# Turning the normalised gate input with DRAM loads and VectorE block transposes instead of TensorE

## The chip, the cores and the metric

The kernel runs on one core of a Trainium2 chip. The metric is the device time of one execution in microseconds (us); the median of several executions is given. A profile of one execution shows what each engine did: PE is TensorE's matmuls, PEld its weight loads, DVE VectorE, ACT ScalarE, POOL GpSimd, SP the engine that issues most transfers.

## The reference

One decoder layer on 1024 prompt tokens and 8 sample tokens, model width 1024. The part that matters here is its end:

```python
    m = (sigmoid(g_a) * (y_a @ w_pa) + sigmoid(g_b) * (y_b @ w_pb))
    h = h + rmsnorm(m @ w_out, post_g)
    e = p @ w_ple
    gate = sigmoid(rmsnorm(h, ple_in_g) @ w_pg)
    h = h + rmsnorm(gate * e, ple_out_g)
    # rmsnorm(x, g) = x * rsqrt(mean(x * x) + EPS) * g, over the 1024 features
```

Before it stand the input projection to seven branches, chunked gating, pooling and the merge. The outputs are `h` and some states.

## The kernel before, in words

All tensors are float32. A product is computed as three TensorE products of parts: each operand is split into a high part (`h` at the end of its name) by ACT and the rest (`l`) by DVE, and `split` issues both. Large products use Strassen's scheme with seven steps, P1 to P7, for a pair of 128-row tiles; each step is twelve matmuls in the last two stages, and the combinations of operands that it needs are named T1 to T4, B11, B21, B22 (of the moving operand) and S1 to S4, A11 and so on (of the stationary one).

The last two stages are the output projection (`outsteps`, the weights `wo`, whose parts are woB11, woT3 and so on) and the gate (`gatesteps`, the weights `wg`). Both go over four pairs of token tiles. The moving operand is the weight matrix, whose seven parts lie in buffers, high and low, for the whole stage (28 buffers). The stationary operand is the activation with its features on partitions: `Turned` reads it from `big`, a tile of 128 partitions x 8 feature blocks x tokens, where block `k` and partition `p` hold one feature. For the output projection that is the merged `m` (tiles `ms`, `mw`); for the gate it is the normalised `h` (tiles `hs`, `hw`). While the last pair of the output projection runs, the wo parts are given up one by one and the wg parts are loaded and split into the free buffers (`turn_over`); some of the sums of wg's blocks were stored in DRAM far earlier by `column_steps` (`wglow`, `wghigh`).

When a pair of the output projection is done, `out_finish` scales each token tile by its norm and the gain row `post`, adds the residual with an accumulating transfer on POOL's queue and stores `h` to DRAM. One step later `gate_norm` takes the mean square of `h` (ACT) and multiplies `h` by the reciprocal root (DVE), giving `hn`, with tokens on partitions. Five steps after that `gate_input` turns `hn` to features on partitions: eight TensorE transposes of 128x128 into PSUM (tiles `pht`), and eight ACT copies into `big` that multiply by the gain `ple_in_g`, held as a column per feature block in `gvec`. The sample tokens (tile `S`, 8 rows) go through `sample_stationary`.

The instructions are not issued in program order. All calls are recorded by `Planner`, which then works out an order for each engine from estimated durations, due times and dependences, and issues that fixed order (`play`); therefore nearly all instructions carry the one line L290, and tile names tell them apart. Loads and intermediate tiles take buffers from one pool of 46 (`slot`). A step has a time `at` which the planner works from; an instruction is not started more than 14 us before it is due, and a transfer on SP's queue keeps its place in SP's order and waits there for what it needs. PSUM has three regions for step results (`acc`, `acct`) and two single banks (`bank`: pht, psst, sps and others).

Of the kernel before, what the change touches and what calls it, by code (L numbers as in the profile page):

```python
# [8 lines left out]
F32 = mybir.dt.float32  # L9
F32R = mybir.dt.float32r  # L10
BF16 = mybir.dt.bfloat16
AF = mybir.ActivationFunctionType
ALU = mybir.AluOpType

P = 128
D = 1024
NB = D // P
SEQ = 1024
NS = 8
T = SEQ + NS  # L20
HALF = 512
QUART = 256
# [274 lines left out]
def hybrid_step(  # L297
# [7 lines left out]
    nc = tc.nc  # L305
    cpool = ctx.enter_context(tc.tile_pool(name="consts", bufs=1))
    spool = ctx.enter_context(tc.tile_pool(name="slots", bufs=SLOTS))
    small = ctx.enter_context(tc.tile_pool(name="small", bufs=20))
    dram = ctx.enter_context(tc.tile_pool(name="spill", bufs=1, space=bass.MemoryType.DRAM))
# [11 lines left out]
    def slot(name, shape=(P, T), dt=F32):  # L321
        n_name[0] += 1
        return plan.tile(spool.tile(list(shape), dt, tag="slot", name=f"{name}_{n_name[0]}", bufs=SLOTS,
                                    padded_shape=None), "slot")
# [5 lines left out]
    def bank(name):  # L330
        n_name[0] += 1
        return plan.tile(bankp.tile([P, 512], F32, tag="bank", name=f"{name}_{n_name[0]}"), "bank")
# [8 lines left out]
    def split(src, hi, lo):  # L341

        nc.scalar.activation(out=hi, in_=src, func=AF.Copy)
        nc.vector.tensor_tensor(out=lo, in0=src, in1=f32(hi), op=ALU.subtract)

    def dma(out, in_, by=None):
        (by or nc.sync).dma_start(out=out, in_=in_)
# [7 lines left out]
    def mul(out, a, b):  # L355
        nc.vector.tensor_tensor(out=out, in0=a, in1=b, op=ALU.mult)
# [9 lines left out]
    nc = plan  # L366
# [37 lines left out]
    class Operand:  # L404
# [37 lines left out]
        def at(self, what, k):  # L442
            return [part[:, k % 2, :] for part in self.parts[what, k // 2]]

    class Stored(Operand):
# [4 lines left out]

        def __init__(self, name, b, low, high, wide=WIDE, free=None):
            super().__init__(name, wide)
            self.src, self.raw, self.free = {"b": b, "low": low, "high": high}, {}, free or {}

        def load(self, what):
            key, i, j = self.ROWS[what]
            first = self.wide if key == "low" else HALF
            c = slice(first, first + self.wide) if j else slice(0, first)
            for kk in range(2):
                r = (4 * i + 2 * kk) * P  # L460
                w = c.stop - c.start
                if what in self.free:
                    raw = self.free[what][:, kk * 2 * w : (kk + 1) * 2 * w].rearrange("p (k t) -> p k t", k=2)
                else:
                    raw = slot(f"{self.name}{what}", (P, 2, w))
                self.raw[what, kk] = raw
                dma(raw, self.src[key][r : r + 2 * P, c].rearrange("(k p) t -> p k t", p=P))

        def cut(self, what):
            for kk in range(2):  # L470
# [202 lines left out]
    class User:  # L673

        func = AF.Copy
# [104 lines left out]
        nc.vector.tensor_tensor(out=low[:NS, :], in0=ps[:NS, :], in1=low[:NS, :], op=ALU.add)  # L780
        return low

    def sample_stationary(src, nk, gain=None):

        st = slot("sst", (P, nk, P), F32R)
        nc.gpsimd.memset(f32(st), 0.0)
        ps = bank("psst").rearrange("p (k t) -> p k t", t=16)
        for k in range(nk):
            nc.tensor.transpose(ps[:, k, :NS], src[:NS, k * P : (k + 1) * P], ident[:NS, :NS])
        got = ps[:, :nk, :NS]  # L790
        if gain is not None:
            mul(smix_s, got, gain.unsqueeze(2).to_broadcast([P, NB, NS]))
            got = smix_s
        split(got, st[:, :, :NS], st[:, :, 32 : 32 + NS])
        return st


# [48 lines left out]
    S = NB  # L846
# [138 lines left out]
    for key, w in (("ya", WIDE), ("yb", WIDE), ("wo", HALF), ("wg", HALF)):  # L985
        kept[key + "low"] = dram.tile([HALF, 2 * w], F32, tag=key + "low", name=key + "low")
        kept[key + "high"] = dram.tile([HALF, HALF + w], F32, tag=key + "high", name=key + "high")
    kept["h"] = dram.tile([T, D], F32, tag="h", name="h")
    kept["e"] = dram.tile([T, D], F32, tag="e", name="e")

    def spill(key, b, src, by=None):
# [19 lines left out]
    def stored(key, src, width, free=None):  # L1011
        return Stored(key, src, kept[key + "low"], kept[key + "high"], width, free)
# [297 lines left out]
    def column_sums(key, src, b):  # L1310

        lo, hi = raw = [slot(f"{key}raw", (P, D)) for _ in range(2)]
        for i, t in enumerate(raw):
            dma(t, src[(4 * i + b) * P : (4 * i + b + 1) * P, :])
        return lambda: store_sums(key, b, lo, hi, HALF)

    def column_steps(key, src, steps):
# [2 lines left out]
            at(l, lambda b=b, held=held: held.append(column_sums(key, src, b)))  # L1320
            at(c, lambda held=held: held[0]())

    for n, (key, src) in enumerate((("wo", w_out), ("wg", w_pg))):
        column_steps(key, src, [(uflow[8 + 5 * (4 * n + i)], uflow[11 + 5 * (4 * n + i)]) for i in range(4)])

    def sample_product(st, op):
# [48 lines left out]
    def gate_norm(t):  # L1375

        r = rows(t)
        h = h_of.pop(t)
        hn = hn_of[t] = slot("hn", (P, D))
        rs = rstd([square_sum(h[:r], r, scratch=hn)], r)  # L1380
        nc.vector.tensor_scalar_mul(hn[:r], h[:r], rs[:r])

    def gate_input(t):

        hn = hn_of.pop(t)
        if t == S:
            samples["h"] = sample_stationary(hn, NB, gvec[:, 2 * NB :])
            return
        for k4 in range(0, NB, 4):
            ps = bank("pht")  # L1390
            for k in range(4):
                nc.tensor.transpose(ps[:, k * P : (k + 1) * P], hn[:, (k4 + k) * P : (k4 + k + 1) * P], ident)
            for k in range(4):
                nc.scalar.activation(out=big[:, k4 + k, t * P : (t + 1) * P], in_=ps[:, k * P : (k + 1) * P],
                                     func=AF.Copy, scale=col(2, k4 + k))

    def merged_sample():
        st = samples["m"] = slot("mst", (P, NB, P), F32R)
# [76 lines left out]
    LAST = ("P1", "P6", "P7", "P4", "P5", "P3", "P2")  # L1475

    FIRST = ("P1", "P7", "P6", "P2", "P4", "P5", "P3")
    woop, wgop = stored("wo", w_out, HALF), stored("wg", w_pg, HALF)
    outsteps = [strassen(Turned(i, "m"), woop, Out(i), Tokens, None if i else FIRST) for i in range(NPAIR)]
    gatesteps = [strassen(Turned(i, "h"), wgop, Embed(i), Tokens, LAST if i == NPAIR - 1 else None)  # L1480
                 for i in range(NPAIR)]
# [10 lines left out]
    def gain_row(key, src):  # L1492
        gains[key] = row_broadcast(src, key)

    at(pbsteps[3][4], lambda: gain_row("post", post_g[0]))
    at(outsteps[3][4], lambda: gain_row("out", ple_out_g[0]))
    at(outsteps[0][1], merged_sample)
    at(outsteps[1][2], out_sample)
# [69 lines left out]
        dma(rows[:, t : t + 2, n * HALF : (n + 1) * HALF], e)  # L1568

    def embed_sample():  # L1570
        st = sample_stationary(praw[2], 2)
        for n in range(2):
            full = sample_matmul([(st[:, k, :], *we.at(n, k)) for k in range(2)])
            dma(kept["e"][SEQ:T, n * HALF : (n + 1) * HALF], full[:NS])


    def begin():

        psl = slot("psamp", (P, PLE))
        p_load(0)  # L1580
        we.fetch(0, nc.scalar)
        for t in range(4):
            x_load(t)
        for i, v in enumerate((pre_g, pool_scale, ple_in_g)):
            dma(vecs[i * NB : (i + 1) * NB, :], v[0].rearrange("(k p) -> k p", p=P), nc.scalar)
        we.fetch(1)
        steps[0].loads()
        dma(xe[:NS], x_sample)
        for t in range(4, NB):
            x_load(t)  # L1590
        p_load(1)
        dma(psl[:NS], p_sample)
        praw.append(psl)
        steps[4].loads()
        fetched[0] = 5
        early_loads()

        plan.fixed = False
        ps = bank("warm")
        for t in range(10):  # L1600
            nc.tensor.transpose(ps[:, t % 4 * P : (t % 4 + 1) * P], ident, ident)
        p_turn(0)
        we_cut(0)
        for t in range(4):
            norm_root(t)
            norm_scale(t)
        embed(0, 0)
        embed_out(0, 0)
        embed(1, 0)
        embed_out(1, 0)  # L1610
        vps = bank("vecs")
        nc.tensor.transpose(vps[:, : 3 * NB], vecs[: 3 * NB, :], ident[: 3 * NB, : 3 * NB])
        nc.vector.tensor_copy(gvec, vps[:, : 3 * NB])
        we_cut(1)
        embed(0, 1)
        embed_out(0, 1)
        x_half(0, (0, 1))
        xop.cut("B11")
        steps[0].prepare()
        embed(1, 1)  # L1620
        embed_out(1, 1)
        x_half(0, (2, 3))
        xop.cut("B21")
        steps[0].run()
        steps[0].evacuate()
        steps[1].prepare()
        norm_root(S)
        norm_scale(S)
        for t in range(4, NB):
            norm_root(t)  # L1630
            norm_scale(t)
        x_extra()
        steps[1].run()
        steps[1].evacuate()
        p_turn(1)
        embed(2, 0)
        embed_out(2, 0)
        x_half(1, (0, 1))
        xop.cut("B12")
        embed(2, 1)  # L1640
        embed_out(2, 1)
        x_half(1, (2, 3))
        xop.cut("B22")
        embed(3, 0)
        embed_out(3, 0)
        prepared[0] = 4
        small_tables()
        steps[2].run()
        steps[2].evacuate()
# [5 lines left out]
        we.drop(0)  # L1655
        we.drop(1)

    gvec = cpool.tile([P, 3 * NB], F32, tag="gvec", name="gvec")
    begin()
    for s in range(3):  # L1660
        for f in steps[s].after:
# [34 lines left out]
```

## Time and profile before

| | |
|---|---|
| time, median of 3 runs | 1005.81 us (1005.71 to 1006.13) |
| profiled execution, its own time: the span from first to last instruction | 1004.0 us; the median of the runs holds 1.8 us more |
| PE busy | 988.3 us in 6186 matmuls |
| DVE busy | 798.0 us in 1239 instructions |
| ACT busy | 489.0 us in 889 instructions |
| POOL busy | 81.0 us in 162 instructions |
| DRAM read, written | 112.49 MB, 47.58 MB |

Busy time is the time in which at least one instruction of the engine is under way; matmuls overlap each other, so their own durations add up to more. In rows of groups the columns are line, engine, operation, output <- inputs, shapes, count | busy us, mean ns of one | idle time before them and what ended it. In rows of a timeline they are start, us, engine, line, operation. In rows of the chain that ended last they are start, us, engine and tile. The output projection runs from about 825 to 907 us, the gate from 900 to the end.

### The profile page before, as it was taken

How to read it: one execution, taken by the hardware profiler on the slowest of the kernel's cores; microseconds unless marked ns; L12 is line 12 of the kernel's file. 1: busy time of each engine (PE TensorE's matmuls, PEld its weight loads, DVE VectorE, ACT ScalarE, POOL GpSimd, SP SyncE). 2: the span in 40 equal slices, each digit the busy share in tenths (PEclk: the TensorE clock that was granted, in tenths of full speed). 3: DMA queues.
4: the chain of work that ended last, by engine and by line, in shares of the span. 5: the costliest groups of instructions: out<-in, count | busy, mean ns of one | idle time of the engine just before them, and what ended most of it. 6: DMA issues, size and time to landing. Idle time of an engine off the chain costs nothing. (4 is left out here: it accounts for less than half of the span.)

```text
span 1004.0 us, 16119 instructions
## 1 busy us (share of the span) xinstructions
PE 988.3 (98%) x6186; PEld 887.4 (88%) x6186; DVE 798.0 (79%) x1239; ACT 489.0 (49%) x889; POOL 81.0 (8%) x162
## 2 busy tenths in 40 slices
PE   8999999999999999999999999999999999998996
PEld 6899999999999999999999999999999988887885
DVE  5697448876779898887776987697799898779796
ACT  7765355555434334232432333562353365678563
POOL 1230001000000000000010100000000002312121
PEclk9999999999999999999999999999999999999998
DMA  9331213222365675441304076973754543397437
GB/s 352 130 107 43 85 43 128 85 85 85 131 225 190 238 269 197 169 169 53 126 13 157 28 251 214 315 281 122 247 218 150 182 152 84 87 306 259 128 75 221
DMA packets 85601, 160.65 MB, mean 160 GB/s; under 512 B 7422, under 2 KB 46382, under 8 KB 85517
## 3 DMA queue, kind: packets, MB, share of 16 engines
q1 hardware_dynamic: 83157, 151.72, 43.1%
q0 software_dynamic: 2048, 7.37, 4.3%
q8 instruction: 48, 0.79, 0.3%
q10 hardware_dynamic: 320, 0.54, 0.2%
q14 instruction: 28, 0.23, 0.1%
HBM read 112.49 MB, written 47.58 MB: 159 GB/s over the span
## 5 line engine op out<-in xcount | busy, mean ns | idle before, releaser
L290 DVE TENSOR_TENSOR u<-acc,u 128x520 f32<-128x520 f32 (+1 forms) x90 | 62.4, 695 | 38.6 <-PE acc L290 34.4
L290 POOL TENSOR_TENSOR rstd<-ms,mhalf 128x1 f32<-128x1 f32 (+1 forms) x45 | 40.7, 907 | 218.4 <-DVE ms L290 196.0
L290 POOL MEMSET u<- 128x8 f32 x35 | 3.7, 105 | 548.9 <-PE acc L290 270.2
L290 ACT ACTIVATE u<-acc 128x512 f32<-128x512 f32 x39 | 23.2, 595 | 35.2 <-PE acc L290 35.0
L290 ACT ACTIVATE paw<-pas 128x512 fp32r<-128x512 f32 x16 | 10.1, 630 | 30.5 <-DVE pas L290 25.2
L290 DVE TENSOR_TENSOR big<-big 128x1024 f32<-128x1024 f32 (+4 forms) x20 | 24.5, 1262 | 0.0
L290 ACT ACTIVATE pbw<-pbs 128x512 fp32r<-128x512 f32 x16 | 10.0, 629 | 28.8 <-DVE pbs L290 25.5
L290 DVE TENSOR_TENSOR xb<-acc,u 128x520 f32<-128x520 f32 (+1 forms) x12 | 8.3, 693 | 19.1 <-PE acc L290 19.1
L290 ACT ACTIVATE zbw<-zbs 128x512 fp32r<-128x512 f32 x16 | 9.9, 628 | 27.4 <-DVE zbs L290 24.1
L290 ACT ACTIVATE big<-vt 128x256 f32<-128x256 f32 x32 | 11.9, 381 | 19.7 <-PE vt L290 19.7
L290 ACT ACTIVATE big<-pht,gvec 128x128 f32<-128x128 f32 x64 | 18.0, 398 | 7.1 <-PE pht L290 7.1
L290 PE MATMUL accm<-qh,wpoolw 128*128 128x260 f32 (+1 forms) x96 | 20.9, 320 | 0.0
L290 ACT ACTIVATE big<-mix 128x256 f32<-128x256 f32 x32 | 12.1, 383 | 17.6 <-PE mix L290 17.2
L290 DVE TENSOR_TENSOR acc<-acc,u 128x512 f32<-128x512 f32 (+1 forms) x16 | 11.2, 697 | 8.8 <-PE acc L290 8.8
L290 ACT ACT_TABLE_LOAD x13 | 16.7, 1283 | 2.6 <-PE acc L290 1.6
L290 DVE TENSOR_TENSOR v<-acc,u 128x520 f32<-128x520 f32 (+1 forms) x9 | 6.2, 693 | 14.4 <-PE acc L290 14.4
L290 PEld LDWEIGHTS accm<-qh,wpoolw 128*128 128x128 f32 x96 | 15.7, 188 | 1.9
L290 ACT ACTIVATE gbw<-gbs 128x512 fp32r<-128x512 f32 x16 | 10.0, 625 | 14.9 <-DVE gbs L290 14.1
L290 ACT ACTIVATE xbw<-xbs 128x512 fp32r<-128x512 f32 x16 | 9.8, 625 | 15.2 <-DVE xbs L290 12.8
L290 DVE SCALAR_TENSOR_TENSOR zb<-accm,gvec,zb 128x512 f32<-128x512 f32 (+1 forms) x16 | 12.0, 751 | 6.5 <-PE accm L290 6.4
L290 DVE TENSOR_TENSOR big<-mix,big 128x256 f32<-128x256 f32 x32 | 13.2, 421 | 4.4 <-ACT big L290 3.6
L290 ACT ACTIVATE uw<-us 128x512 fp32r<-128x512 f32 x16 | 9.8, 628 | 13.5 <-DVE us L290 7.6
(689 smaller groups left out, 3622.2 us busy)
## 6 DMA issues: line engine op xcount, KB each, us to landing
ga<-ga SPq DMA_DIRECT2D x16, 516.0 KB
gb<-gb SPq DMA_DIRECT2D x16, 516.0 KB
ya<-za SPq DMA_DIRECT2D x8, 516.0 KB
yb<-zb SPq DMA_DIRECT2D x8, 516.0 KB
x<-in_x_prompt_dram SPq DMA_DIRECT2D x8, 512.0 KB
vraw<-in_w_in_dram SPq DMA_DIRECT2D x8, 512.0 KB
e<-e SPq DMA_DIRECT2D x8, 512.0 KB
garaw<-in_w_in_dram SPq DMA_DIRECT2D x8, 512.0 KB
```

What stands on the lines that cost most here:

```text
L290: getattr(getattr(self.nc, e), method)(*args, **kwargs)
```

## The change: what it does

`hn` of a prompt tile is multiplied by the root and by the gain in one DVE instruction, with the gain as a row on all partitions (`gains["in"]`, loaded once), and stored to DRAM (`kept["hn"]`). `gate_input` loads it back with four transfers; transfer `j` takes 256 features of the 128 tokens and puts token block `b` (32 tokens each) and token `i` of it at partition `32 j + i`, column block `b`. One DVE instruction then transposes all blocks of 32x32 in place of the 64 TensorE transposes of the eight tiles, writing straight to `big`. Since partition `p` then holds the features `8 p + k`, and no longer `k * 128 + p`, the gate's weights are read with their rows in the same order: `w_gate` is `w_pg` seen as `(p k) m -> p k m`. The sample tile's features are taken in steps of eight, and its gain multiplication in `sample_stationary` goes. The column form of `ple_in_g` goes from `vecs` and `gvec`.

```diff
@@ class Stored
         def __init__(self, name, b, low, high, wide=WIDE, free=None):
             super().__init__(name, wide)
-            self.src, self.raw, self.free = {"b": b, "low": low, "high": high}, {}, free or {}
+            chunks = lambda src: src.rearrange("(k p) t -> p k t", p=P)
+            self.src = {"b": b if len(b.shape) == 3 else chunks(b), "low": chunks(low), "high": chunks(high)}
+            self.raw, self.free = {}, free or {}
...
-                r = (4 * i + 2 * kk) * P
+                r = 4 * i + 2 * kk
...
-                dma(raw, self.src[key][r : r + 2 * P, c].rearrange("(k p) t -> p k t", p=P))
+                dma(raw, self.src[key][:, r : r + 2, c])
@@ sample_stationary
-    def sample_stationary(src, nk, gain=None):
+    def sample_stationary(src, nk):
...
-            nc.tensor.transpose(ps[:, k, :NS], src[:NS, k * P : (k + 1) * P], ident[:NS, :NS])
-        got = ps[:, :nk, :NS]
-        if gain is not None:
-            mul(smix_s, got, gain.unsqueeze(2).to_broadcast([P, NB, NS]))
-            got = smix_s
-        split(got, st[:, :, :NS], st[:, :, 32 : 32 + NS])
+            nc.tensor.transpose(ps[:, k, :NS], src[:NS, k], ident[:NS, :NS])
+        split(ps[:, :nk, :NS], st[:, :, :NS], st[:, :, 32 : 32 + NS])
...
+    kept["hn"] = dram.tile([SEQ, D], F32, tag="hn", name="hn")
@@ column_sums
-            dma(t, src[(4 * i + b) * P : (4 * i + b + 1) * P, :])
+            dma(t, src[:, 4 * i + b])
...
-    for n, (key, src) in enumerate((("wo", w_out), ("wg", w_pg))):
+    w_gate = w_pg.rearrange("(p k) m -> p k m", k=NB)
+    for n, (key, src) in enumerate((("wo", w_out.rearrange("(k p) m -> p k m", p=P)), ("wg", w_gate))):
@@ gate_norm
-        nc.vector.tensor_scalar_mul(hn[:r], h[:r], rs[:r])
+        nc.vector.scalar_tensor_tensor(out=hn[:r], in0=h[:r], scalar=rs[:r], in1=gains["in"][:r],
+                                       op0=ALU.mult, op1=ALU.mult)
+        if t != S:
+            dma(kept["hn"][t * P : (t + 1) * P, :], hn)
@@ gate_input
         if t == S:
-            samples["h"] = sample_stationary(hn, NB, gvec[:, 2 * NB :])
+            samples["h"] = sample_stationary(hn.rearrange("p (f k) -> p k f", k=NB), NB)
             return
-        for k4 in range(0, NB, 4):
-            ps = bank("pht")
-            for k in range(4):
-                nc.tensor.transpose(ps[:, k * P : (k + 1) * P], hn[:, (k4 + k) * P : (k4 + k + 1) * P], ident)
-            for k in range(4):
-                nc.scalar.activation(out=big[:, k4 + k, t * P : (t + 1) * P], in_=ps[:, k * P : (k + 1) * P],
-                                     func=AF.Copy, scale=col(2, k4 + k))
+        blocks = slot("hq", (P, 4, QUART))
+        src = kept["hn"][t * P : (t + 1) * P, :].rearrange("(b i) f -> i b f", i=32)
+        for j in range(4):
+            dma(blocks[32 * j : 32 * j + 32], src[:, :, j * QUART : (j + 1) * QUART])
+        nc.vector.transpose(out=big[:, :, t * P : (t + 1) * P].rearrange("p k (b i) -> p k b i", i=32),
+                            in_=blocks.rearrange("p b (r k) -> p k b r", k=NB))
...
-    woop, wgop = stored("wo", w_out, HALF), stored("wg", w_pg, HALF)
+    woop, wgop = stored("wo", w_out, HALF), stored("wg", w_gate, HALF)
...
+    at(outsteps[0][1], lambda: gain_row("in", ple_in_g[0]))
@@ begin
-        for i, v in enumerate((pre_g, pool_scale, ple_in_g)):
+        for i, v in enumerate((pre_g, pool_scale)):
...
-        nc.tensor.transpose(vps[:, : 3 * NB], vecs[: 3 * NB, :], ident[: 3 * NB, : 3 * NB])
-        nc.vector.tensor_copy(gvec, vps[:, : 3 * NB])
+        nc.tensor.transpose(vps[:, : 2 * NB], vecs[: 2 * NB, :], ident[: 2 * NB, : 2 * NB])
+        nc.vector.tensor_copy(gvec, vps[:, : 2 * NB])
...
-    gvec = cpool.tile([P, 3 * NB], F32, tag="gvec", name="gvec")
+    gvec = cpool.tile([P, 2 * NB], F32, tag="gvec", name="gvec")
```

More of the change, by code (lines that the diff above doesn't have):

```diff
@@ L1570, in embed_sample @@
     def embed_sample():
-        st = sample_stationary(praw[2], 2)
+        st = sample_stationary(praw[2].rearrange("p (k c) -> p k c", k=2), 2)
         for n in range(2):
```

## The prediction

> **What bounds the kernel now.** I read the page's busy times first.
>
> ```profile
> span 1004.0 us, 16119 instructions
> PE 988.3 (98%) x6186; PEld 887.4 (88%) x6186; DVE 798.0 (79%) x1239; ACT 489.0 (49%) x889; POOL 81.0 (8%) x162
> ```
>
> TensorE (PE) is busy for 98% of the span, so a matmul taken off it is worth its full time unless another engine is just behind. All times below are made against this execution: span 1004.0 us, and the median of 1005.81 us holds 1.8 us more around it. Anything within 0.2% (2.0 us) of that median counts as no change here.
>
> Next, the windows of time around the part that the change touches (us; busy PE, PEld, DVE, ACT, POOL with instruction counts; granted clock; DMA share; GB/s). I cut it where the character changes and call the first three A, B and C.
>
> ```profile
> 840.00:903.00 63.00, 63.00 (x300) 51.57 (x299) 47.89 (x79) 44.78 (x108) 16.97 (x20) 1.00 0.67 186
> 903.00:925.00 22.00, 19.20 (x86) 14.97 (x85) 21.44 (x28) 20.17 (x40) 5.88 (x6) 1.00 0.92 307
> 925.00:960.00 35.00, 35.00 (x161) 28.63 (x160) 26.89 (x44) 19.23 (x48) 5.85 (x6) 1.00 0.35 92
> ```
>
> In A and C PE never pauses (63.00 of 63.00, 35.00 of 35.00). VectorE (DVE) has 63.00 - 47.89 = 15.1 us idle in A and 8.1 us in C. In B it is the other way: DVE is busy 21.44 of 22.00 and PE pauses for 2.8 us. The chain of waits and the waits of PE say the same thing:
>
> ```profile
> PE acct L290 <- DVE ms L290: 1.6, 1, 1.6
> PE acct L290 <- DVE hw L290: 1.2, 1, 1.2
> ```
>
> ```profile
> 917.39 2.27 DVE wgT1l L290 x2
> ...
> 920.87 1.19 DVE wgB22l L290 x2
> ...
> 924.48 3.02 PE acct L290 x12
> 927.50 0.87 PE pht L290 x8
> 928.37 2.78 PE acct L290 x12
> ```
>
> The chain runs through DVE's splits of the gate weights (wgT1l, wgB22l) up to 924.48, and from there through PE, with the transposes `pht` as links of 0.87 us per group of eight. So the bound is PE, except for B, which is the turnover from the output projection to the gate: there it is DVE.
>
> **What is removed.** Eight token tiles lose eight TensorE transposes each, with the ACT copies that empty them.
>
> ```profile
> L290 PE MATMUL pht<-ident,hn x64: 270/272/277, 856.7 to 931.7; 128*128 128x128 f32 x64
> L290 ACT ACTIVATE big<-pht,gvec x64: 359/390/483, 857.4 to 933.8; 128x128 f32<-128x128 f32 x64
> ```
>
> ```profile
> 840.00:903.00 63.00, 5.18 (x40) 4.68 (x40) 10.57 (x38) 1.00 0.67 186
> 903.00:925.00 22.00, 1.04 (x8) 0.94 (x8) 3.02 (x12) 1.00 0.92 307
> 925.00:960.00 35.00, 2.07 (x16) 1.86 (x16) 4.41 (x16) 1.00 0.35 92
> ```
>
> The 272 ns of one are pipelined; what a group of eight adds to the stream is the 0.87 us of the chain, 109 ns each. The last three rows are the same windows for `pht` alone (PE, PEld, ACT): 5 groups in A, 1 in B, 2 in C. That is 4.35, 0.87 and 1.74 us of PE, 6.96 in all. ACT loses 18 us of busy time, 3.0 of them in B, where it was at 20.17 of 22.00. The gain multiplication that rode on these copies moves to DVE; one 128x64 multiplication and split step of the sample rows gets shorter, which I count as nothing.
>
> **What is added on DVE.** Per tile one transpose of 128x1024, and the normalisation becomes a three-operand instruction, as the one for `post` already is.
>
> ```profile
> L290 DVE SCALAR_TENSOR_TENSOR h<-h,rstd,post 128x1024 f32<-128x1024 f32 x8 | 10.3, 1283 | 3.5 <-POOL rstd L290 3.5
> L290 DVE TENSOR_SCALAR hn<-h,rstd 128x1024 f32<-128x1024 f32 x8 | 6.0, 746 | 0.5 <-POOL rstd L290 0.5
> ```
>
> ```profile
> 837.78 1.28 DVE L290 SCALAR_TENSOR_TENSOR h<-h,rstd,post 128x1024 f32<-128x1024 f32 x1
> 838.98 0.20 DVE L290 TENSOR_SCALAR ms<-ssq,ssq 128x1 f32<-128x1 f32 x1
> ...
> 897.46 0.75 DVE L290 TENSOR_SCALAR hn<-h,rstd 128x1024 f32<-128x1024 f32 x1
> 898.12 1.22 DVE L290 TENSOR_TENSOR wgT2l<-wgT,wgT2h 128x1024 fp32r<-128x1024 f32 x1
> 899.25 0.69 DVE L290 TENSOR_TENSOR hw<-hs,hw 128x512 fp32r<-128x512 f32 x1
> ```
>
> ```profile
> 840.00:903.00 63.00, 4.46 (x6) 1.00 0.67 186
> 903.00:925.00 22.00, 0.75 (x1) 1.00 0.92 307
> 925.00:960.00 35.00, 1.49 (x2) 1.00 0.35 92
> ```
>
> Neighbours overlap a little, so I price by the distance from start to start where nothing waits: 838.98 - 837.78 = 1.20 for the new form against 898.12 - 897.46 = 0.66 for the old, +0.54 a tile. The last three rows are DVE's instructions on `hn`: six in A (one is the sample tile), one in B, two in C.
>
> No DVE transpose is in this trace. From below I take the 0.66 us of the one-tensor instruction on `hn`, from above twice the 1.13 us (899.25 - 898.12) of the two-tensor subtraction, if a block had to be filled before it is drained or the read in steps of eight floats ran at half rate: 2.26 us. I take 1.13, because a transpose that streams reads and writes each element once, like that row. [...]
>
> So the eight transposes cost 9.0 us of DVE, the nine normalisations 4.9. In A come four transposes (tiles 0 to 3) and six normalisations: 4.5 + 3.2 = 7.7 us. In B one normalisation, 0.54. In C two normalisations and four transposes: 1.1 + 4.5 = 5.6 us. Tiles 4 and 5 are normalised just before and in B, but first used by the third pair of the gate, so their transposes can fall behind B; if they don't, B gets 2.26 more.
>
> **What is added on the queues.** Per tile one store of 512 KB and four loads of 128 KB on SP's queue, where `hn` stayed on the core before; and once a 512 KB gain row. The path from `hn` to the gate's input gets a DRAM round trip (rows of the tile `hn`, of the transfers, of SP's waits and of the timelines of SP, ACT and PE):
>
> ```profile
> L290 DVE TENSOR_SCALAR hn<-h,rstd x8: 733/748/752, 849.3 to 927.5; 128x1024 f32<-128x1024 f32 x8
> h<-in_x_prompt_dram POOLq DMA_DIRECT2D x8, 512.0 KB, 6.3
> SPq L290 <- PE acct L290: 21.8, 7, 11.1
> 878.97 0.93 SPq L290 DMA_DIRECT2D wgB<-in_w_pg_dram  x2
> 900.59 1.63 SPq L290 DMA_DIRECT2D wgB<-in_w_pg_dram  x2
> 887.93 2.04 ACT L290 ACTIVATE wgB11h<-wgB 128x1024 fp32r<-128x1024 f32 x2
> 900.74 0.47 PE L290 MATMUL acct<-wgB11h,hw 128*128 128x512 f32 x1
> 916.64 2.10 ACT L290 ACTIVATE wgB22h<-wgB 128x1024 fp32r<-128x1024 f32 x2
> ```
>
> By the 6.3 us that a 512 KB transfer takes on POOL's queue, the only one with a time to landing here, store plus loads are some 12 us. Tiles 0 and 1 are normalised from 849 on and needed at 900.74, so the trip is hidden for them, and for the later tiles by the pairs in between. But the loads wait on SP for the store, and the store for DVE; behind them on SP stand the loads of the gate's weights. These have cover: the first is issued at 878.97, split from 887.93 on and used at 900.74; the last is issued at 900.59 and split at 916.64. They also wait for buffers: SP's 21.8 us behind PE's `acct` are loads whose buffer a matmul still reads. The gain row holds one of the 46 buffers from the output projection to the last normalisation, the landing tile another for some us. If this holds the turnover up, it is by at most one PE step, the 2.78 us of the chain, since each step of the output projection frees four buffers; at least nothing. I take 1.0, nearer to nothing because of that cover.
>
> **The sum.** In A, PE gains 4.35. DVE's idle time shrinks by that to 10.75 us and has to take 7.7, which leaves 3.0. It can be filled nearly whole:
>
> ```profile
> 830.00:840.00 10.00, 10.00 (x45) 8.15 (x44) 9.93 (x19) 5.23 (x12) 1.35 (x2) 1.00 0.00 0
> ```
>
> In the 10 us before A, DVE is busy 9.93 and PE does not pause. But the idle time in A is waits on ACT and POOL in an order fixed beforehand, so I take 0.8 lost. If only half of the 15.1 us can be used, 7.7 + 4.35 - 7.55 = 4.5 are lost. In B the end is set by DVE: removing a group of transposes only lengthens PE's pause, and the normalisation adds 0.54. Bounds: -3.7, if ACT's 3.0 freed us let DVE end the pause and the group counts; +2.8, with two transposes. In C PE gains 1.74, DVE's 5.6 go into 8.1 - 1.74 = 6.4 idle: 0 lost, at most the 1.74. Behind 960 nothing is changed. Together -4.35 + 0.8 + 0.54 - 1.74 + 1.0 = -3.75 us: the profiled execution at 1000.25, the median at 1002.1.
>
> **Rivals.**
> 1. DVE takes PE's place (slower). For it: B is bound by DVE already, and 13.9 us are added where 15.1 + 0.6 + 8.1 are idle and PE wants 7.0 back. With half of A's idle time usable, A ends at +0.15, B at +2.8, C at -1.74, buffers +1.0: +2.2, so 1008.0. With a transpose of 2.26 us, A needs 12.3 where 10.75 are left and loses 1.5 besides the 0.8 (-2.05), B +0.54, C has 10.1 for 6.4 (+3.7 - 1.74), buffers 1.0: +1.5, 1007.3. It decides when DVE's losses over the three stages pass 6.1 us, the gain of the seven groups that count. Against it: the 9.93 of 10 us above. [...]
> 2. The pin (no change): B starts when it did, since the weights' loads keep their due times, and A's gain turns into idle time. -1.74 + 0.54 + 1.0 = -0.2: 1005.6. Against it: the loads wait for buffers that PE frees, and so move with PE.
> 3. The weights come late (slower). In B the queues are at a share of 0.92 and 6.8 MB; two tiles' round trips add 2.1 MB, 30%, some 6.7 us. It decides where the slip passes the cover of 9 to 16 us between load and split, with a stall on SP on top. Then those 6.7 us come on the sum: 1008.8.
> 4. All of it is kept and more: the 6.96 us, 998.9, and with ACT's relief also PE's pause of 2.8: 996.1.
>
> **Chances.** The forecast 0.46 (own range 999.4, if A and the buffers lose nothing and B's group counts, to 1003.8, where no change begins), rival 4 0.14, rival 2 0.11, rival 1 0.20, rival 3 0.09. Faster is 0.46 + 0.14 = 0.60, same 0.11, slower 0.29. The range of 998.0 to 1009.0 cuts off the lower part of rival 4 and the upper bounds of rivals 1 and 3.
>
> **What would show it.** Right: no `pht`; PE at about 981 us of busy time; eight DVE transposes at 1.1 to 1.3 us each; DVE idle in what was A down to 2 to 4 us; a PE pause around the gate's first weights of 3 to 6 us, behind DVE. Wrong: transposes of over 2 us; a PE pause that ends with ACT or a DMA of wg parts (rival 3); PE pauses spread through the output projection with DVE full (rival 1); no pause at all (rival 4).

## The result and the profile after

The changed kernel takes 1016.27 us (median of 4 runs, 1015.09 to 1018.17) against 1005.79 us before (median of 4 runs, measured beside it): a ratio of 1.0102, 95% interval 1.009 to 1.0114. The forecast was 1002.1 us, faster; the change is 10.5 us slower and lies 7 us above the upper end of the range. The profiled execution has a span of 1013.4 us. The first two lines of its page:

```profile
span 1013.4 us, 16021 instructions
PE 988.3 (98%) x6122; PEld 883.5 (87%) x6122; DVE 817.9 (81%) x1246; ACT 474.1 (47%) x825; POOL 74.8 (7%) x162
```

PE has 64 instructions less and the same busy time as before, 988.3 us. The transposes were worth 7.0 us of it, so the remaining matmuls took 7.0 us longer. And the time in which PE does nothing went from 1004.0 - 988.3 = 15.7 to 1013.4 - 988.3 = 25.1 us: 9.4 us of new pauses. The span grew by -7.0 + 7.0 + 9.4 = 9.4 us. The 7.0 is eight groups at the 0.87 us of the prediction. The same windows as in the prediction show where (us; PE, PEld, DVE, ACT, POOL; granted clock; DMA share; GB/s):

```profile
0.00:840.00 840.00, 836.48 (x5491) 764.11 (x5492) 668.31 (x1032) 384.65 (x650) 42.55 (x122) 1.00 0.46 157
840.00:903.00 63.00, 61.73 (x270) 49.83 (x269) 53.06 (x77) 37.72 (x74) 12.54 (x17) 1.00 0.73 202
903.00:925.00 22.00, 18.55 (x67) 13.77 (x65) 18.31 (x21) 10.78 (x15) 4.86 (x6) 0.84 1.05 360
925.00:960.00 35.00, 29.71 (x119) 23.03 (x119) 30.45 (x44) 16.94 (x34) 5.64 (x8) 0.95 0.70 191
```

Up to 840 PE pauses 3.5 us, hardly different from the 3.9 before. In A to C it pauses 1.3 + 3.4 + 5.3 = 10.0 us, before 2.8. Behind 960, where the prediction had nothing changed, it is busy for 41.85 of 53.4 us, before for 35.03 of 44.0: another 2.6 us of pauses. Over these windows DVE is not full: it is idle for 9.9 us in A, 3.7 in B and 4.6 in C. The granted clock, 1.00 in all three before, is 0.84 in B. PE's longest waits in these stages:

```profile
PE acct L290 <- ACT hw L290: 2.8, 2, 2.3
PE acct L290 <- DVE wgT3l L290: 2.0, 1, 2.0
PE acct L290 <- DVE wgT1l L290: 1.9, 1, 1.9
PE acct L290 <- DVE hw L290: 1.3, 2, 0.9
PE acct L290 <- DVE h L290: 1.3, 1, 1.3
PE acct L290 <- ACT u L290: 1.2, 1, 1.2
```

They stand behind the splits of the gate's weights and operands, a step late each time, and behind evictions. The chain of waits is of no use here: it holds only the last few us. The granted clock behind three pauses, first PE's timeline (start, us, what; in brackets the pause before it):

```profile
907.92 0.49 PE L290 MATMUL acct<-wgT3h,hw 128*128 128x512 f32 x1 [0.49 <-ACT hw L290]
910.43 0.80 PE L290 MATMUL acct<-wgT3l,hw 128*128 128x512 f32 x1 [2.02 <-DVE wgT3l L290]
912.17 1.22 PE L290 MATMUL acct<-wgT3h,hw 128*128 128x512 f32 x2 [0.94 <-DVE hw L290]
```

and then two windows of 5 us (PE's busy time alone; clock; DMA share; GB/s):

```profile
905.00:910.00 5.00, 2.93 (x12) 1.00 1.04 398
910.00:915.00 5.00, 3.62 (x8) 0.53 1.07 307
```

Pauses of 0.49, 2.02 and 0.94 us within some 5 us are followed by a clock of 0.53: eight matmuls start in 5 us, where an undisturbed 10 us (830 to 840 in the prediction) hold 45. It does not take several pauses: the one of 1.92 us before 927.01 is the first since 912.17, and the matmuls behind it start 0.43 us apart, where 0.23 is usual. The same holds behind the pause of 2.30 us before 959.85, with one of 0.38 us before 960.96 behind it, but not behind those of 1.27 (898.81) and 1.22 us (966.32). By an estimate from the granted clock in B and C, 18.55 x 0.16 + 29.71 x 0.05 = 4.5 of the 7.0 us that PE was to win went here; the other 2.5 I did not place. What decides whether the clock falls behind a pause, no run here shows.

Why the splits are late: first the groups of the new DVE instructions (busy us, mean ns), then ACT's waits for transfers, then the issues with their time to landing (last number, us), and a row of SP's waits.

```profile
L290 DVE STREAM_TRANSPOSE big<-hq 128x1024 f32<-128x1024 f32 x8 | 17.3, 2162 | 2.7 <-DMA hq<-hn 2.7
L290 DVE SCALAR_TENSOR_TENSOR hn<-h,rstd,in 128x1024 f32<-128x1024 f32 x8 | 10.2, 1277 | 1.7 <-POOL rstd L290 1.7
```

```profile
ACT wgB11h L290 <- DMA wgB<-in_w_pg_dram: 4.3, 1, 4.3
ACT wgT2h L290 <- DMA wgT<-wglow: 2.8, 1, 2.8
```

```profile
hn<-hn SPq DMA_DIRECT2D x8, 512.0 KB, 2.6
hq<-hn SPq DMA_DIRECT2D x32, 128.0 KB, 5.5
wgB<-in_w_pg_dram SPq DMA_DIRECT2D x6, 512.0 KB, 9.3
wgT<-wghigh SPq DMA_DIRECT2D x4, 512.0 KB, 10.6
```

```profile
SPq L290 <- DVE hn L290: 35.3, 6, 14.3
```

A transpose takes 2.16 us, not 1.13. The gate's weights take 9.3 to 10.6 us to land, and ACT, which never waited for them before, waits 7.1 us. But that is not what most of PE's pauses come from. ACT splits the weights at most 0.4 us later than before, most of them earlier, except for wgB22, and there it had waited 7.6 us for DVE's `ge`. For wgT1 its group in the kernel before and in the changed one:

```profile
L290 ACT ACTIVATE wgT1h<-wgT x2: 1152/1152/1153, 913.7 to 914.7; 128x1024 fp32r<-128x1024 f32 x2
L290 ACT ACTIVATE wgT1h<-wgT x2: 1041/1041/1041, 909.7 to 910.6; 128x1024 fp32r<-128x1024 f32 x2
```

What the engines did ahead of the three longest pauses (rows of the changed kernel's timelines):

```profile
907.96 1.28 DVE L290 SCALAR_TENSOR_TENSOR hn<-h,rstd,in 128x1024 f32<-128x1024 f32 x1 [1.23 <-POOL rstd L290]
909.16 2.35 DVE L290 TENSOR_TENSOR wgT3l<-wgT,wgT3h 128x1024 fp32r<-128x1024 f32 x2
916.87 1.22 DVE L290 TENSOR_TENSOR wgT1l<-wgT,wgT1h 128x1024 fp32r<-128x1024 f32 x1
918.60 2.22 DVE L290 STREAM_TRANSPOSE big<-hq 128x1024 f32<-128x1024 f32 x1
923.70 2.15 DVE L290 STREAM_TRANSPOSE big<-hq 128x1024 f32<-128x1024 f32 x1
925.76 1.20 DVE L290 TENSOR_TENSOR wgT1l<-wgT,wgT1h 128x1024 fp32r<-128x1024 f32 x1
927.01 0.55 PE L290 MATMUL acct<-wgT1l,hw 128*128 128x512 f32 x1 [1.92 <-DVE wgT1l L290]
934.24 14.98 SPq L290 DMA_DIRECT2D hn<-hn  x2
949.40 3.87 SPq L290 DMA_DIRECT2D hq<-hn  x4
957.08 2.05 DVE L290 STREAM_TRANSPOSE big<-hq 128x1024 f32<-128x1024 f32 x1 [2.65 <-DMA hq<-hn]
959.17 0.63 ACT L290 ACTIVATE hw<-big 128x512 fp32r<-128x512 f32 x1 [3.63 <-DVE big L290]
959.85 0.50 PE L290 MATMUL acct<-wgB11h,hw 128*128 128x512 f32 x1 [2.30 <-ACT hw L290]
```

The pause of 2.02 us ends with the split of wgT3: on DVE it stood behind a normalisation that had waited 1.23 us for its root. The pause of 1.92 us ends with the second half of wgT1's split: between its halves DVE ran two transposes, 4.4 us, and other work without a gap. The pause of 2.30 us is the round trip's own. SP's order has the store of a later tile ahead of the loads of the fifth tile (counted by the issues), and that store waits 14.3 of SP's 35.3 us for its `hn`; so the loads are issued at 949.40, DVE waits for them, ACT for DVE's transpose, and PE for ACT. The last loads of the gate's weights, by contrast, are issued at 899.79, before at 900.59. Only the pause of 1.27 us at 898.81 goes back to a load of weights: ACT waits 2.8 us for wgT2, DVE 2.0 for ACT, and the eviction `h` that PE needs stands behind it.

### The profile page after: what moved, and what is told of

It reads as the page before. It is cut to its first block, busy times and chain, and to the rows that moved or that the text cites. A ratio compares the mean times of both kernels' runs of the same rounds, so it can differ in the third digit from the quotient of the medians.

```text
span 1013.4 us, 16021 instructions
## 1 busy us (share of the span) xinstructions
PE 988.3 (98%) x6122; PEld 883.5 (87%) x6122; DVE 817.9 (81%) x1246; ACT 474.1 (47%) x825; POOL 74.8 (7%) x162
## 5 line engine op out<-in xcount | busy, mean ns | idle before, releaser
L290 POOL TENSOR_TENSOR rstd<-ms,mhalf 128x1 f32<-128x1 f32 (+1 forms) x45 | 34.7, 789 | 205.5 <-DVE ms L290 183.1
L290 ACT ACTIVATE junk<-ge 128x512 bf16<-128x512 f32 (+2 forms) x19 | 11.5, 608 | 22.0 <-DVE ge L290 21.6
L290 DVE STREAM_TRANSPOSE big<-hq 128x1024 f32<-128x1024 f32 x8 | 17.3, 2162 | 2.7 <-DMA hq<-hn 2.7
```

The lines of the kernel that those rows point to most:

```text
L290: getattr(getattr(self.nc, e), method)(*args, **kwargs)
```

## The experiments

All medians stand beside the kernel before on the same chip (1005.9 to 1006.6 us); ratios are to it, with the 95% interval. Besides the whole time I compare the length of the last two stages in the profiled executions: from the first matmul on woB11h, with which the output projection starts (810.4 in the kernel before, earlier than the 825 given further up), to the end of the span. The groups of these matmuls (ns of one, smallest, median and largest; first and last start) in the kernel before:

```profile
L290 PE MATMUL acct<-woB11h,mw x32: 387/392/482, 810.4 to 882.2; 128*128 128x512 f32 x32
```

in the changed kernel:

```profile
L290 PE MATMUL acct<-woB11h,mw x32: 388/394/400, 808.2 to 877.7; 128*128 128x512 f32 x32
```

in e16, a kernel told of below:

```profile
L290 PE MATMUL acct<-woB11h,mw x32: 388/392/477, 819.7 to 891.4; 128*128 128x512 f32 x32
```

and in e18:

```profile
L290 PE MATMUL acct<-woB11h,mw x32: 388/392/399, 822.3 to 891.8; 128*128 128x512 f32 x32
```

With their spans of 1004.0, 1013.4, 1013.8 and 1026.5 us these are 193.6, 205.2, 194.1 and 204.2 us. The others are worked out in the same way. Each is one execution, and not always a typical one: e15's is its slowest, 3.7 us above its median.

| kernel | median, us | ratio, interval | last two stages, us |
|---|---|---|---|
| before | 1005.8 | | 193.6 |
| changed | 1016.27 | 1.0102 (1.009 to 1.0114) | 205.2 |
| e1 transposes only | 1012.48 | 1.0057 (1.0042 to 1.0072) | 200.9 |
| e2 round trip only | 1020.66 | 1.0141 (1.0126 to 1.0156) | 207.7 |
| e4 told the price | 1017.77 | 1.012 (1.0101 to 1.0139) | 207.3 |
| e5 contiguous read | 1010.65 | 1.0047 (1.003 to 1.0064) | 198.4 |
| e6 e5, ACT's queue | 1024.21 | 1.0176 (1.0159 to 1.0194) | 212.1 |
| e7 gain row only | 1009.75 | 1.0031 (1.0019 to 1.0043) | 196.8 |
| e8 quarter of the bytes | 1013.18 | 1.0071 (1.005 to 1.0091) | 200.7 |
| e9 e5, own buffer | 1011.59 | 1.005 (1.0035 to 1.0065) | 198.1 |
| e10 e5, gain in weights | 1017.96 | 1.0114 (1.0096 to 1.0133) | 201.4 |
| e11 e5, SBUF blocks | 1036.27 | 1.0301 (1.0284 to 1.0318) | 224.4 |
| e12 e10 and e11 | 1039.5 | 1.0336 (1.0321 to 1.0352) | 225.3 |
| e13 no turning | 1001.96 | 0.9962 (0.9947 to 0.9977) | 190.8 |
| e14 blocks for 4 tiles | 1011.63 | 1.0058 (1.004 to 1.0076) | 200.1 |
| e15 blocks for 2 tiles | 1012.36 | 1.0059 (1.0036 to 1.0082) | 204.7 |
| e16 before, 13 us | 1015.62 | 1.0097 (1.008 to 1.0114) | 194.1 |
| e17 before, DVE price | 1009.49 | 1.003 (1.0019 to 1.0041) | 194.2 |
| e18 changed, 13 us | 1028.09 | 1.0218 (1.0193 to 1.0243) | 204.2 |
| e19 e5, 13 us | 1023.64 | 1.0162 (1.014 to 1.0184) | 199.7 |

Theory 1 was that DVE's time decides, theory 2 the DRAM round trip (2a its place in SP's order, 2b its bytes, 2c its buffers), theory 3 an order worked out from a wrong price, theory 4 that any new order costs some us.

**The transposes alone (e1).**

```diff
 gate_input of the kernel before, after its ACT copies
+        scratch = slot("hq", (P, D))
+        nc.vector.transpose(out=scratch.rearrange("p (k b i) -> p k b i", k=NB, i=32),
+                            in_=hn.rearrange("p (b r k) -> p k b r", k=NB, b=4))
```

> The kernel before, with the eight VectorE transposes of hn added (read in steps of eight floats, as the change does), into a buffer that nobody reads; TensorE's transposes, the copies, the normalisation and the transfers stay as before. Theory 1 (VectorE's time decides: a transpose takes 2.16 us, not 1.13): VectorE gets 17 us more around the turnover from the output projection to the gate, TensorE pauses there for 6 to 12 us, 1010 to 1016 us. Theory 2 (the DRAM round trip decides: transfers, their place in SP's order, buffers): the transposes fall mostly into idle time, 1006 to 1008 us. Both: each transpose takes 2.0 to 2.3 us.

1012.48 us: 5.9 more, as theory 1 has it. PE pauses behind a late normalisation (PE's waits in e1):

```profile
PE pht L290 <- DVE hn L290: 3.6, 2, 3.2
PE sps L290 <- DVE slow L290: 2.0, 1, 2.0
```

**The round trip alone (e2).**

```diff
 gate_norm, gate_input of the kernel before
-        nc.vector.tensor_scalar_mul(hn[:r], h[:r], rs[:r])
+        nc.vector.scalar_tensor_tensor(out=hn[:r], in0=h[:r], scalar=rs[:r], in1=gains["in"][:r],
+                                       op0=ALU.mult, op1=ALU.mult)
+        if t != S:
+            dma(kept["hn"][t * P : (t + 1) * P, :], hn)
...
+        blocks = slot("hq", (P, 4, QUART))
+        src = kept["hn"][t * P : (t + 1) * P, :].rearrange("(b i) f -> i b f", i=32)
+        for j in range(4):
+            dma(blocks[32 * j : 32 * j + 32], src[:, :, j * QUART : (j + 1) * QUART])
```

> The kernel before, with the rest of the change added: gain row, three-operand normalisation, the store of hn and the four block loads a tile into a buffer that nobody reads; TensorE still transposes hn and ScalarE copies it to the gate's input without the gain. Theory 1: VectorE gets only 5 us more, 1006 to 1009 us. Theory 2: the gate's weights come later than before and TensorE pauses behind them, 1010 to 1016 us, with waits of ScalarE for transfers of the gate's weights as in the changed kernel (4.3 and 2.8 us there).

1020.66 us: 14.0 more, above what theory 2 expected. The waits of e2 between 900 and 945 us:

```profile
ACT hn L290 <- DMA hq<-hn: 8.2, 1, 8.2
PE acct L290 <- DVE wgT1l L290: 6.5, 1, 6.5
DVE wgT1l L290 <- DMA hq<-hn: 6.1, 1, 6.1
```

DVE's split of wgT1 waits 6.1 us for a block load to land, and PE 6.5 us for the split. The split does not read that load; it writes a buffer that the load had, so 2b and 2c meet in this wait. It belongs to e2: nobody reads the loaded tile there, and its buffer comes free with the landing. In the changed kernel the transposes read it, and no split waits for such a load. The sign that theory 2 named, ACT's waits for the gate's weights, is smaller here (2.1 and 1.1 us) than in the changed kernel, while SP issues the last of these loads at 908.63, later than there. So either part alone costs time, the round trip more, but the 14.0 us are not its price inside the change.

**Told the price (e4).** In the planner's estimate: `if method == "transpose": return 0.065 + n * 0.00205`.

> The changed kernel, with one edit in the planner: it counts a VectorE transpose of 1024 columns at 2.16 us, as measured, and no longer at 1.14, and orders the engines by that. Theory 3 (the loss is in an order worked out from a wrong price): the transposes move out of the way of the weights' splits, TensorE's pauses shrink by half or more, 1005 to 1010 us. Theories 1 and 2: the load is the same and only the order differs, 1013 to 1018 us.

1017.77 us, no better. Theory 3 falls for this price; the planner's estimates for transfers were not varied.

**Contiguous read (e5).**

```diff
-    w_gate = w_pg.rearrange("(p k) m -> p k m", k=NB)
+    w_gate = kept["wgp"]    # [P, NB, D], filled early:
+        for j in range(4):
+            dma(kept["wgp"][32 * j : 32 * j + 32],
+                w_pg[j * QUART : (j + 1) * QUART].rearrange("(k r) m -> r k m", k=NB))
...
-                            in_=blocks.rearrange("p b (r k) -> p k b r", k=NB))
+                            in_=blocks.rearrange("p b (k r) -> p k b r", k=NB))
```

> The changed kernel with another order of features: partition 32 j + r holds features 256 j + 32 k + r, so that the VectorE transpose reads 32 neighbouring floats instead of 32 in steps of eight. The gate's weights are brought into that order once, by four DRAM to DRAM transfers early in the kernel; the sample tile gets one small copy. If the step of eight is what doubles the transpose, it takes 1.1 to 1.3 us here; if a transpose of float32 takes two passes anyway, 2.0 to 2.3. Theory 1: with 1.2 us, VectorE has 8 us less and the time falls to 1002 to 1008 us. Theory 2: the round trip is unchanged, 1012 to 1017 us whatever the transpose takes.

The group of its transposes:

```profile
L290 DVE STREAM_TRANSPOSE big<-hq 128x1024 f32<-128x1024 f32 x8 | 9.9, 1234 | 1.7 <-DMA hq<-hn 1.7
```

1010.65 us, 5.6 less than the change and between the ranges of the two theories; 4.0 us of loss are left against the kernel before. The transpose takes 1.234 us: the step of eight floats in the read costs the other 0.93 us, 0.9 ns for each element, and eight of them are 7.4 us of DVE. The contiguous read takes about as long as the two-tensor subtraction of the same size (1.22 us, the row at 916.87 of the changed kernel). Why a step costs that much, no run here shows.

**Whose queue, whose buffer (e6, e9), and what else is in the round trip (e7, e8).** e6 puts `nc.scalar` as the issuer into the store and the four loads of e5. e9 replaces the landing tile of e5 by `blocks = hn.rearrange("p (b f) -> p b f", b=4)`. e7 is e2 without the store and the loads. e8 is e2 with

```diff
-            dma(kept["hn"][t * P : (t + 1) * P, :], hn)
+            dma(kept["hn"][t * P : t * P + 32, :], hn[:32])
...
-            dma(blocks[32 * j : 32 * j + 32], src[:, :, j * QUART : (j + 1) * QUART])
+            dma(blocks[32 * j : 32 * j + 32, :1], src[:, :1, j * QUART : (j + 1) * QUART])
```

> The kernel with the contiguous read (e5, 1010.65 us), with the store of hn and the four block loads a tile issued on ScalarE's queue and no longer on SP's. Theory 2a (order: on SP's queue the loads of the gate's weights stand behind loads that wait for a store): SP's waits for hn disappear, the weights come earlier, 1005 to 1008 us. Theory 2b (bytes: the transfers are full between 885 and 930 us) and 2c (buffers): 1009 to 1012 us, with the transfers' share there still at 1.0 or above.

> The kernel of e2 (1020.66 us) without the store and the block loads: against the kernel before only the gain row, which holds a buffer, and the three-operand normalisation remain, and the ScalarE copies have no gain. If the round trip itself makes e2's 14 us, 1005 to 1008 us. If the buffer of the gain row or VectorE's 5 us make them (2c), over 1010 us.

> The kernel of e2 with the same number of stores, loads and waits, but a quarter of the bytes in each (32 of the 128 tokens are stored and loaded; what is loaded is not read, as in e2). Theory 2b (bytes): the loss against the kernel before falls from 14 to 2 to 5 us, 1008 to 1011 us. Theories 2a and 2c (order and buffers): 1015 to 1021 us.

> The kernel with the contiguous read (e5), whose block loads land in the buffer of hn itself, free once the store is done, and not in one of their own. Theory 2c (buffers: the landing tile takes one where the gate's weights wait for theirs): 1005 to 1008 us. Theories 2a and 2b: 1009 to 1012 us.

The gain row and the normalisation cost 3.1 us (e7, between its two ranges). So the round trip as e2 has it costs 14.0 - 3.1 = 10.9, and with a quarter of the bytes 6.6 - 3.1 = 3.5 us (e8, between its two ranges as well): 7.4 us hang on the bytes. On ACT's queue it gets worse by 13.6 us (e6), and ACT, which splits, then stands still itself: before `hw` it waits 12.3 us for a store of the output, and PE 14.4 us for ACT (e6's waits):

```profile
PE acct L290 <- ACT hw L290: 14.4, 1, 14.4
ACT hw L290 <- DMA out_dram<-ge: 12.3, 1, 12.3
```

The landing tile's own buffer makes no difference (e9), at least beside the contiguous read.

**Trying to save what the parts cost (e10 to e12).** e10 takes e5, lets ACT multiply the rows of `w_pg` by the gain where `column_sums` loads them, stores them to `kept["wgp"]`, and drops the gain row and the three-operand form. e11 takes e5 and replaces store and loads by

```diff
+        for j in range(4):
+            for b in range(4):
+                dma(blocks[32 * j : 32 * j + 32, b], hn[32 * b : 32 * b + 32, j * QUART : (j + 1) * QUART])
```

e12 is both.

> The kernel with the contiguous read (e5, 1010.65 us), with the gain ple_in_g multiplied into the rows of the gate's weights by ScalarE, early, where they are loaded for the block sums anyway; they are then stored in DRAM in the order of features that the transpose gives, and loaded from there. So there is no gain row and no three-operand normalisation. By e7 (3.1 us over the kernel before for these two), 1006 to 1009 us if the parts add up. If VectorE is not what the rest waits for, 1010 to 1012 us.

> The kernel with the contiguous read (e5), whose blocks are placed by sixteen transfers a tile from hn straight into the landing tile, in place of one store and four loads through DRAM: half the bytes and one trip instead of two, but 128 issues instead of 40. Theory 2b (bytes, and e8 says that they are about half of the round trip's loss): 1004 to 1008 us. Theory 2a (order on SP's queue): the issues, at about 0.35 us each, hold the weights up more, 1011 to 1016 us.

> Both edits of e10 and e11 on the kernel with the contiguous read. If they add up, 1001 to 1006 us, the first version of the change that is not slower than the kernel before.

All three are far worse. In e11 the issue is the price. One takes 0.59 us at the median (e11's group of them on SP), and the 32 of two tiles need 22 us of SP's timeline, the first time with the weights' loads behind them:

```profile
L290 SPq DMA_DIRECT2D hq<-hn x128: 507/589/1656, 862.1 to 998.0; - x128
```

```profile
862.07 21.61 SPq L290 DMA_DIRECT2D hq<-hn  x32
```

The first of these loads is issued at 885.04, where it was 878.97 before, and the transposes themselves wait 19.0 us for their blocks. So 2a is real once there are enough issues. In e10 PE already loses 2.8 us between 300 and 420, where the weights are now stored, and then 7.2 us behind `hw`; why that many I did not settle.

**No turning (e13).** In `gate_input` of the kernel before, all transposes of the prompt tiles and all but one copy of 128 columns a tile are left out.

> The kernel before without turning the prompt tiles at all: TensorE's 64 transposes and all but one small ScalarE copy a tile are left out, so that the gate reads for the prompt what lies in its input buffer. It bounds what the change can win. By the prediction's step (0.87 us for each of the seven groups that count, or of all eight, and TensorE's pause of 2.8 us between the stages gone or kept): 996 to 1000 us. If the pause grows where the transposes go, because VectorE is the bound there, 1001 to 1004 us.

The head of its page:

```profile
span 1001.2 us, 15954 instructions
PE 983.0 (98%) x6122; PEld 881.4 (88%) x6122; DVE 797.9 (80%) x1239; ACT 475.2 (47%) x833; POOL 78.7 (8%) x162
```

1001.96 us: 3.9 us less, of 7.0. In the profiled execution, its slowest, PE's busy time falls by 5.3 us only, at a mean granted clock of 0.993 against 0.997, and its idle time rises from 15.7 to 18.2. That is about what any way of turning could win here; it is no strict bound, since the planner draws a new order for this kernel, too.

**Out of the turnover (e14, e15).** The changed kernel with TensorE transposes, of `hn.rearrange("p (f k) -> p k f", k=NB)[:, k]`, for tiles 2 to 5 (e14), or 0 to 5 (e15).

> The changed kernel, with the block way only for tiles 0, 1, 6 and 7; tiles 2 to 5, which fall into the turnover from the weights of the output projection to those of the gate, are turned by TensorE in the same order of features (read in steps of eight). Gain row and three-operand normalisation stay. Theory 2b (bytes while the transfers are full, 885 to 930 us): 2.1 of the 4.2 MB of loads and stores that fell there, and four slow transposes, are gone, 1006 to 1010 us. If the place of the bytes does not matter, half of the change's loss stays, plus TensorE's 3.5 us, 1012 to 1016 us.

> The same with the block way for tiles 6 and 7 alone, which are needed last. By e7 the gain row and the normalisation cost 3.1 us; the last pair's round trip lies behind the turnover, where the transfers' share was 0.35 and VectorE had 8 us idle in 35: theory 2b 1007 to 1010 us, about as e7 with less TensorE work and reading in steps of eight.

1011.63 and 1012.36 us, both above what the bytes theory expected (e14 just below its rival's range), the second with no gain from taking out two more tiles. In e15's profiled execution PE pauses 5.7 us behind `ge` and 3.2 behind wgT4l. So 2b, as I had put it, is not shown: bytes count (e8), but not simply where the transfers are full. TensorE's weight load for `pht` pays for the step of eight as well. The groups in e14,

```profile
L290 PEld LDWEIGHTS pht<-ident,hn x32: 185/190/207, 876.8 to 910.5; 128*128 128x128 f32 x32
```

and in the kernel before:

```profile
L290 PEld LDWEIGHTS pht<-ident,hn x64: 138/140/144, 856.5 to 931.6; 128*128 128x128 f32 x64
```

A group of eight loses little by it: PE's timeline has 1.04 us for the one at 909.87 in e14, and 1.03 for the one at 885.17 before.

**Another order for the same work (e16 to e19).** In the planner `LEAD` is 13.0 for 14.0 (e16 on the kernel before, e18 on the changed one, e19 on e5); e17 counts 0.075 for 0.065 in VectorE's fixed price.

> The kernel before with the same work, but the planner may start an instruction 13 us ahead of its due time, not 14: another order, nothing else. Theory 4 (the order of the kernel before is a lucky or chosen one for its planner's constants, and any edit draws a new one that costs some us): 1008 to 1012 us. If the order has little weight: 1005 to 1007 us.

> The kernel before with the same work, but the planner counts 0.010 us more for every VectorE instruction. As e16: theory 4 1008 to 1012 us, otherwise 1005 to 1007 us.

> The changed kernel with the planner's 13 us. If the change's loss is its own work and bytes: 1013 to 1020 us, 8 us or more over e16. If it is mostly the draw of the order: it can come out near e16, 1008 to 1013 us.

> The kernel with the contiguous read (e5, 1010.65 us) with the planner's 13 us. If the 5.6 us between e5 and the changed kernel come from the transposes' 0.93 us each, it stays about that far under e18, whatever the order: 1006 to 1014 us. If they were a draw, the two change places or meet.

e16 is 9.3 us slower than the kernel before with the same work, more than theory 4 expected, e17 3.1. So far theory 4 holds. But the place of that loss is another: in e16 and e18 alike PE waits 6.1 us early in the kernel, in the sample's mixing (e16's waits; e18 has the same row),

```profile
PE smix L290 <- DVE sv L290: 6.1, 1, 6.1
```

and the last two stages take 194.1 and 194.2 us, as before (193.6). There the changed kernel has 205.2 and 204.2, and the contiguous read 198.4 and 199.7, under either constant. So in these stages another order with the same work moves the time by 0.5 to 1.3 us in the four pairs tried, the change costs 10 to 12 us, and 4.5 to 6.8 of them are the step of eight. By the medians e18 lies 12.5 us over e16 and 4.5 over e19, so both losses stay under the other order, though e18 and e19 lie above all the ranges given for them.

## Why the prediction was wrong, point by point

- **The bound.** Reading A and C as bound by PE was right in the trace and wrong as a price. "Worth its full time unless another engine is just behind": another one was. Without any turning the kernel wins 3.9 us (e13), where the sum had 4.35 + 1.74 for seven groups.
- **The transpose.** The term that was mis-sized most plainly: 1.13 us taken, 2.16 measured, near the upper end of 2.26. The reason named for that end, a read in steps of eight, is the one that e5 shows. At 1.234 us the change is still slower by 4.0 us (e5).
- **The idle time in A.** The sum put four transposes and six normalisations there and none of the transposes into B. In the changed kernel two transposes and five normalisations ran in A (DVE 53.06 of 63 us, and PE's pause of 1.3 us is near the 0.8 of the sum). Two transposes, started at 918.60 and 923.70, fell into B and between the halves of a split, one into C, and three behind 960, where the sum had none. So A's idle time was not what failed, but the place of the work.
- **The normalisation.** +0.54 us held (1277 ns against 746). Gain row and normalisation together cost 3.1 us (e7).
- **The queues.** The step that failed furthest: the round trip was taken as hidden by the pairs in between, and transfers put at nothing, with 1.0 us for buffers, on account of a cover of 9 to 16 us between load and split. Added to the kernel before, it costs 10.9 us (e2 against e7, with e2's own wait for a buffer in it); inside the change no run has it alone. The cover of the weights held but for one pause of 1.27 us, although they take 9.3 and 10.6 us to land. What had no cover is the trip of `hn` itself in SP's order: the loads of the fifth tile stood behind a store that waited 14.3 us, and PE paused 2.30 us for them.
- **The clock** was in none of the steps. In B and C it took back some 4.5 us of PE's time, against 6.96 that the transposes were worth.
- **The rivals.** Rival 1 came, without the full DVE that was its sign, and of rival 3 the full transfers and SP's stall, but hardly the late weights. With the right transpose, rival 1 gave 1007.3, and rival 3 gave 1008.8 with the sum's own transpose; each was priced with the other absent, and the range ended at 1009.0. The parts measured alone, -3.9 (e13), +5.9 (e1) and +14.0 (e2), add up to +16.0, where the change has +10.5: they do not simply add, which would fit pauses that they share and the wait that only e2 has.
- **The signs.** No `pht`: right. PE at 981 us: wrong, 988.3. Transposes of over 2 us and pauses of PE spread over the stage: the signs given for rival 1, though DVE was not full. ACT waits for wg transfers, but no long pause of PE ends there, and ACT waits 2.9 us for them in e13 as well, without any round trip: that sign does not tell.

Open: why taking the round trip out of the stretch of full transfers (e14, e15) leaves 5.5 to 6.2 us, what the round trip costs inside the change, and why folding the gain (e10) loses.

## What to carry to other kernels

Before pricing work that is taken off the busiest engine, ask what else would be late by that much: leave the work out altogether once, and see what is left of the gain. The transpose that was moved here from TensorE to VectorE had its data placed across partitions by a round trip first, and that round trip, added alone, cost 10.9 us (e2 against e7), where TensorE's transposes were worth 7.0 us of PE; ask of each of its loads what stands ahead of it in its queue and what that waits for. When a fixed order is worked out by a planner, change one of its constants with the work unchanged: it showed 3 to 9 us here, and comparing the length of the touched stages instead of whole times told that apart from the change.

## What the runs showed of the hardware

- A step of eight floats (32 bytes) in the read: the VectorE transpose of 128x1024 takes 2.16 us in the changed kernel, for 1.23 in e5, and TensorE's weight load of 128x128 takes 190 ns in e14, for 140 before, though a group of eight takes 1.04 us for 1.03.
- In the changed kernel pauses of PE of 1.92, 2.02 and 2.30 us are followed by matmuls that start 0.43 us apart, for 0.23 (about the 2.02 and behind the 2.30 there are shorter pauses too; behind the 2.02 the granted clock is 0.53 over 5 us); behind pauses of 1.22 and 1.27 us the 0.23 stays.
- An issue on SP's queue takes 0.59 us in the middle for the 32 KB transfers from SBUF to SBUF of e11, and 0.43 for the 128 KB block loads from DRAM in the changed kernel:

```profile
L290 SPq DMA_DIRECT2D hq<-hn x32: 302/430/2182, 859.4 to 963.8; - x32
```
